# Token mixer: six of eight input tiles in the output product's first pass, one of its columns earlier, and the 32-row gate product ahead of the RWKV sums

## The chip, the cores and the metric

The kernel runs on one core of one Trainium2 chip. The time is the device time of one launch in microseconds (us), and the median of several runs counts. All operands are fp32; sequence length T is 512 and the width D is 1024.

## The reference, cut to what matters

Two hybrid layers (chunked attention and retention) come first, then one block of FFN, token mixer and FFN. The change lies in the token mixer alone:

```python
def token_mixer(u, w_in, w_out, ...):          # u: (1, 512, 1024), normalised
    p = u @ w_in
    p_pool, p_hg, p_rw, p_gla = jnp.split(p, ...)
    y_pool = causal_multiscale_pool(p_pool, ...)                 # 256 channels
    y_hgrn = rms_norm_2(gated_linear_attention(...)) * sigmoid(hg)
    y_rwkv = (group_norm(rwkv7_scan(...)) + bonus) * g_r
    log_a = log_sigmoid(ga @ gla_w2 + gla_b) / 16                # ga: 16 of the columns of p_gla
    y_gla  = rms(gated_linear_attention(..., log_a)) * silu(gg)
    y = concatenate([y_pool, y_hgrn, y_rwkv, y_gla])             # 4 x 256 channels
    return y @ w_out

x = x + token_mixer(rms_norm(x), ...)
x = x + 0.5 * swiglu_ffn(rms_norm(x), ...)
```

## The kernel before, in words

**Products.** A tile holds 128 channels by 512 tokens, so x and y are eight tiles each. Every big product is made in split precision: ScalarE (ACT) casts the 128-column fp32 weight to `whi` (L192), VectorE (DVE) subtracts to give the rest `wlo` (L193), and the input has the parts z0h, z0l, z1h and so on. For each of the eight input tiles TensorE (PE) then runs three matmuls (`mm3`: L214 high by high, L215 high by low, L216 low by high), so that a product of 128 output columns is 24 matmuls. Its result lies in one of three PSUM banks `mm`, and DVE reads it out.

**Mixer.** The four groups are written as generators: RWKV halves `r0` and `r1`, gated linear attention (GLA) halves `g0` and `g1`, HGRN `h`, pooling `p`, and the output product `o`. MIX_ORDER is the list in which their steps are emitted. A scheduler then lays the instructions out in one queue for each engine; each engine works through its queue in order. The products of the mixer's input (matmuls on z0h ... z7l) are the filler among the short, dependent steps of the groups.

**RWKV.** For each half, `pw` (L889) and `pa` (L894) are products with 64 contraction rows, `ss` (L930, L931) are sums over the head dimension as matmuls with 2 output columns. A solve of seven levels then goes through a DMA (`LQ` to `pr`, `zz`, L1021, L1023) and alternates PE products (L1005) with DVE or ACT copies; `pWU` (L1052) follows it, then a scan over the chunks, and `pO` (L1123) makes the half's output in PSUM. DVE takes BN statistics of pO (L1129, L1130), makes 1/sqrt in ten tiny steps (L232 to L243) and `bnm` (L1135); ACT scales (`on`, L1138, eight instructions); DVE finishes it (L1140, L1142), PE transposes it (`pt`, L1145) and L1146 gives the tile `gr`.

**GLA gate.** The first step of `g0` makes the product of columns 3216 to 3344, reads 32 rows of it into `ga`, and multiplies these with `wl2` (`pz`, L1293, 32 contraction rows, two results of 512 tokens).

**Pooling.** For each of its two channel tiles, DVE scales the product's result into `pp` (L767), GpSimd (POOL) builds the trailing windows in tiles `s` by copies and adds (L1410, L1411, L1423; five instructions for the first channel tile, nine for the second), DVE finishes them (L1425 to L1427), PE multiplies (`pm`, L1430), and DVE adds bias and scale (L1431).

**Output product** (`mix_out`). It splits the first W_EARLY tiles of W_ORDER (y tiles 0, 1 are pooling, 2, 3 HGRN, 4, 5 RWKV, 6, 7 GLA) into `ysh` (ACT, L204) and `ysl` (DVE, L205), reloads x by POOL's queue (L835), and then goes twice over the eight output columns. The first pass takes the early tiles, the second the rest, each with its own weight DMAs, `whi` cast and `wlo` subtraction, and after each column DVE adds the PSUM result to x (L862). In the second pass each x tile is also squared (L255 on ACT), added to `nacc` (DVE, L257) and split into the next FFN's inputs (z parts, L207 on ACT and L208 on DVE). The FFN's first products follow, and need all eight z tiles.

Of the kernel before, what the change touches and what calls it, by code (L numbers as in the profile page):

```python
# [25 lines left out]
MAGIC = 12582912.0  # L26
NBT = 15
NBU = 17
MIX_ORDER = ("r0 r0 g0 r0 g0 g0 r0 r0 g0 r0 g0 r0 r0 g1 r0 g0 g1 r1 g1 r1 r1 r1 h r1 r1 r1 g1 r1 h h h h g1 g1 h "
             "r1 p p h h o o o o o h h h o o o o")  # L30
W_ORDER = (6, 7, 0, 1, 4, 5, 2, 3)
W_EARLY = 4
MIX_BANKS = (0, 1, 2, 2)

VEC_WIDTHS = [
# [81 lines left out]
class Build:  # L117
# [552 lines left out]
    def mixer(self):  # L670
# [5 lines left out]
        with ExitStack() as ctx:  # L676
# [135 lines left out]
            def go(g, n=1):  # L812
                for _ in range(n):
                    r = next(g, None)
                    if r is not None:
                        y.update(r)

            wo = self.mix_out(y, xs)
            gens = {"r0": rw[0], "r1": rw[1], "g0": gl[0], "g1": gl[1], "h": hg, "p": po, "o": wo}
            for step in MIX_ORDER.split():  # L820
                go(gens[step])
# [3 lines left out]
    def mix_out(self, y, xs):  # L825
# [4 lines left out]
        t32r = lambda part: self.mp.tile([128, T], F32R, tag="t", name="ys" + part, bufs=NBT)  # L830
        for c in W_ORDER[:W_EARLY]:
            sp[c] = self.split(y[c], alloc=t32r)
        for c in range(ND):
            x[c] = self.xp.tile([128, T], F32, tag="x", name="x")
            nc.gpsimd.dma_start(out=x[c], in_=xs[c])  # L835
        for ks in (W_ORDER[:W_EARLY], W_ORDER[W_EARLY:]):
            last = ks[-1] == W_ORDER[-1]
# [686 lines left out]
```

## Time and profile before

| | |
|---|---|
| median of 3 runs | 1649.86 us (1648.52 to 1650.13) |
| profiled execution, its own time | 1650.48 us |
| its span | 1648.7 us |
| PE busy | 1607.0 us, 97% of the span |
| DVE busy | 1025.3 us, 62% |
| ACT busy | 649.1 us, 39% |
| POOL busy | 130.0 us, 8% |
| mean granted TensorE clock | 0.993 of full |

The profile is one execution; its times are counted from the start of its span. The execution's own time is 1.8 us more than the span (launch and end). In rows of the timeline the first number is the start, the second the time that the instruction (or the run of `xN` like ones) took; a bracket gives the idle time ahead of it on its engine and what released it. The granted clock is 1.00 for TensorE's 2.4 GHz and 0.50 for its 1.2 GHz. A matmul's time includes the filling of the pipeline, so that dense 512-column matmuls take 0.39 us each in a row but start every 0.23 us.

### The profile page before, as it was taken

Reading aid. Unit: us, or ns where it says so; the run is one execution under the profiler, and the core shown is the slowest. Engines: PE = TensorE matmul, PEld = TensorE weight load, DVE = VectorE, ACT = ScalarE, POOL = GpSimd, SP = SyncE. Lnnn points to the kernel's source line nnn. Section 1 sums busy time; section 2 is a strip of 40 time slices with the busy share of each in tenths; the row PEclk is TensorE's granted clock in tenths of the full one; section 3 lists DMA queues with packets and bytes.
Section 4 is the critical chain, followed back from the end, with each engine's and each line's share of the span. In section 5 each row is a group of like instructions: output and inputs, shape, how many; then the busy total and the mean of one; then the engine's idle time right before and its main releaser. Section 6 shows DMA issues by size and latency. Waiting matters only on the chain.

```text
span 1648.7 us, 23282 instructions
## 1 busy us (share of the span) xinstructions
PE 1607.0 (97%) x9160; PEld 1296.8 (79%) x9160; DVE 1025.3 (62%) x2044; ACT 649.1 (39%) x1125; POOL 130.0 (8%) x108
## 2 busy tenths in 40 slices
PE   8988999999999999999999999999989999999998
PEld 6766888877788888888888877777767888888886
DVE  6787766577876775555533377779888554544232
ACT  5654424365533533223223226337445232322321
POOL 0396020000011000000000000000200000000000
PEclk9999999999999999999999999999999999999999
DMA  6322222433223223333333432212013333332331
GB/s 211 85 76 60 74 73 83 118 87 86 72 66 92 77 83 97 103 90 102 96 107 114 122 99 68 56 40 62 25 57 114 108 95 101 91 103 87 102 96 61
DMA packets 270669, 145.76 MB, mean 88 GB/s; under 512 B 10576, under 2 KB 265312, under 8 KB 270560
## 3 DMA queue, kind: packets, MB, share of 16 engines
q1 hardware_dynamic: 265600, 138.89, 29.1%
q0 software_dynamic: 1280, 4.20, 0.8%
q10 hardware_dynamic: 3680, 1.19, 0.3%
q8 instruction: 72, 1.18, 0.3%
q14 instruction: 37, 0.30, 0.1%
HBM read 139.80 MB, written 4.46 MB: 87 GB/s over the span
## 4 chain that ended last, share of the span: by engine, by line
PE 61%; DVE 4%; ACT 2%; issue 0%; DVEq 0%; ACTq 0%
PE mm L214 18%; PE mm L216 18%; PE mm L215 18%; DVE xr L1225 1%; PE po L1269 0%; DVE wlo L193 0%; PE pO L1123 0%; PE pLQ L954 0%; DVE pr L1021 0%; PE bc L281 0%; DVE X L1217 0%; DVE X L1221 0%; PE pWU L1052 0%; PE pT L1005 0%; DVE zz L1023 0%
## 5 line engine op out<-in xcount | busy, mean ns | idle before, releaser
L192 ACT CAST whi<-wraw 128x1024 fp32r<-128x1024 f32 (+2 forms) x260 | 261.8, 1008 | 702.7 <-PE mm L215 477.7
L193 DVE TENSOR_TENSOR wlo<-wraw,whi 128x1024 fp32r<-128x1024 f32 (+2 forms) x260 | 307.4, 1184 | 157.3 <-ACT whi L192 156.1
L625 DVE SCALAR_TENSOR_TENSOR fa<-mm,R 128x512 f32<-128x512 f32 x44 | 30.3, 691 | 107.8 <-PE mm L216 107.8
L621 DVE SCALAR_TENSOR_TENSOR fa<-mm,R 128x512 f32<-128x512 f32 x44 | 30.3, 691 | 90.4 <-PE mm L216 89.1
L214 PE MATMUL mm<-z0h,whi 128*128 128x512 f32 x179 | 73.1, 408 | 9.1 <-ACT z0h L207 5.7
L214 PE MATMUL mm<-z1h,whi 128*128 128x512 f32 x179 | 71.5, 399 | 0.3 <-ACT z1h L207 0.3
L216 PE MATMUL mm<-z4h,wlo 128*128 128x512 f32 x179 | 71.2, 398 | 0.0
L216 PE MATMUL mm<-z1h,wlo 128*128 128x512 f32 x179 | 71.2, 398 | 0.0
L215 PE MATMUL mm<-z6l,whi 128*128 128x512 f32 x179 | 71.0, 397 | 0.0
L215 PE MATMUL mm<-z3l,whi 128*128 128x512 f32 x179 | 71.0, 396 | 0.0
L215 PE MATMUL mm<-z0l,whi 128*128 128x512 f32 x179 | 70.9, 396 | 0.0
L214 PE MATMUL mm<-z2h,whi 128*128 128x512 f32 x179 | 70.9, 396 | 0.0
L215 PE MATMUL mm<-z2l,whi 128*128 128x512 f32 x179 | 70.8, 395 | 0.1
L214 PE MATMUL mm<-z6h,whi 128*128 128x512 f32 x179 | 70.8, 396 | 0.0
L215 PE MATMUL mm<-z7l,whi 128*128 128x512 f32 x179 | 70.8, 395 | 0.0
L214 PE MATMUL mm<-z3h,whi 128*128 128x512 f32 x179 | 70.7, 395 | 0.0
L215 PE MATMUL mm<-z1l,whi 128*128 128x512 f32 x179 | 70.7, 395 | 0.0
L215 PE MATMUL mm<-z5l,whi 128*128 128x512 f32 x179 | 70.7, 395 | 0.0
L216 PE MATMUL mm<-z5h,wlo 128*128 128x512 f32 x179 | 70.6, 394 | 0.0
L216 PE MATMUL mm<-z0h,wlo 128*128 128x512 f32 x179 | 70.6, 394 | 0.0
L216 PE MATMUL mm<-z2h,wlo 128*128 128x512 f32 x179 | 70.6, 394 | 0.0
L216 PE MATMUL mm<-z3h,wlo 128*128 128x512 f32 x179 | 70.5, 394 | 0.0
(706 smaller groups left out, 4016.4 us busy)
## 6 DMA issues: line engine op xcount, KB each, us to landing
wraw<-in_w_in SPq DMA_DIRECT2D x90, 512.0 KB, 4.1
wraw<-in_ffn_w_in SPq DMA_DIRECT2D x88, 512.0 KB, 3.8
wraw<-in_ffn_w_out SPq DMA_DIRECT2D x32, 512.0 KB, 4.2
wraw<-in_w_out SPq DMA_DIRECT2D x16, 512.0 KB, 4.3
wraw<-in_ffn_w_out SPq DMA_DIRECT2D x16, 384.0 KB, 3.5
bias<-in_relb SPq DMA_DIRECT2D x16, 256.0 KB, 3.1
x<-in_xT SPq DMA_DIRECT2D x8, 256.0 KB, 6.0
xs<-x POOLq DMA_DIRECT2D x8, 256.0 KB, 2.5
```

The costliest lines, as they stand in the source:

```text
L192: nc.scalar.copy(hi[:, ks, :], raw[:, ks, :])
L193: nc.vector.tensor_tensor(out=lo[:, ks, :], in0=raw[:, ks, :], in1=hi[:, ks, :].bitcast(F32), op=ALU.subtract)
L214: mm(out, lhsT=lh, rhs=rh, start=start, stop=False)
L215: mm(out, lhsT=lh, rhs=rl, start=False, stop=False)
L216: mm(out, lhsT=ll, rhs=rh, start=False, stop=stop)
L621: nc.vector.scalar_tensor_tensor(out=a2, in0=pg, scalar=0.5, in1=R, op0=ALU.mult, op1=ALU.mult)
L625: nc.vector.scalar_tensor_tensor(out=a2, in0=pu, scalar=0.5, in1=R, op0=ALU.mult, op1=ALU.mult)
L1225: nc.vector.tensor_tensor(out=yr[o, h, :].rearrange("p (n m) -> p n m", m=m), in0=vw(xx)[o, :, 1, :], in1=vw(q)[o, :, 1, :], op=mult)
```

## The change

W_EARLY goes from 4 to 6: the first pass now takes the two RWKV tiles too (18 matmuls a column, weights of 128x768 elements), and the second only the two HGRN tiles (6 a column, weights of 128x256). All columns together have the same 192 matmuls as before, 144 and 48 instead of 96 and 96. In MIX_ORDER one `o` moves ahead of the two `h` behind the pooling steps, and the first `g0` moves ahead of the second and third `r0`.

```diff
-MIX_ORDER = ("r0 r0 g0 r0 g0 g0 r0 r0 g0 r0 g0 r0 r0 g1 r0 g0 g1 r1 g1 r1 r1 r1 h r1 r1 r1 g1 r1 h h h h g1 g1 h "
-             "r1 p p h h o o o o o h h h o o o o")
+MIX_ORDER = ("r0 g0 r0 r0 g0 g0 r0 r0 g0 r0 g0 r0 r0 g1 r0 g0 g1 r1 g1 r1 r1 r1 h r1 r1 r1 g1 r1 h h h h g1 g1 h "
+             "r1 p p o h h o o o o h h h o o o o")
 W_ORDER = (6, 7, 0, 1, 4, 5, 2, 3)
-W_EARLY = 4
+W_EARLY = 6
```

The first place is PE's queue at the mixer's start. Before, the two `pz` come three product matmuls after the last `ss`:

```order
L931 MATMUL ss<-selrk,rkk 128x2
L930 MATMUL ss<-sel,kk_8035 128x2
L931 MATMUL ss<-selrk,rkk 128x2
L216 MATMUL mm<-z3h,wlo 128x512
L214 MATMUL mm<-z4h,whi 128x512
L215 MATMUL mm<-z4l,whi 128x512
L1293 MATMUL pz<-ga,wl_7848 128x512 x2
L216 MATMUL mm<-z4h,wlo 128x512
```

In the changed kernel they stand in the middle of a product, 44 product matmuls ahead of `pw` and 70 ahead of the first `ss`:

```order
L214 MATMUL mm<-z1h,whi 128x512
L1293 MATMUL pz<-ga,wl_7848 128x512 x2
L215 MATMUL mm<-z1l,whi 128x512
L216 MATMUL mm<-z1h,wlo 128x512
L214 MATMUL mm<-z2h,whi 128x512
L215 MATMUL mm<-z2l,whi 128x512
```

The `ss` keep their neighbours, full product matmuls, and lose `pz`.

The second place is PE's and DVE's queue around the second RWKV half's `pO`. In PE's queue before, both `pm` (s_10677 of the first pooling channel tile, s_10723 of the second) stand right at `pO`, and 14 matmuls of the last HGRN product stand behind:

```order
L1430 MATMUL pm<-s_10677,pw 128x512
L1123 MATMUL pO<-S,RH 64x64 x14
L1123 MATMUL pO<-KV,MN 64x64 x16
L1123 MATMUL pO<-X,LQ 64x64 x16
L1430 MATMUL pm<-s_10723,pw 128x512
L784 MATMUL pv<-cst,hv 128x128 x4
L215 MATMUL mm<-z3l,whi 128x512
```

In the changed kernel 17 product matmuls stand behind `pO`, and they are the end of the second pooling channel's own input product (its `pp` is made from them). These are the last three of them, with what follows:

```order
L214 MATMUL mm<-z7h,whi 128x512
L215 MATMUL mm<-z7l,whi 128x512
L216 MATMUL mm<-z7h,wlo 128x512
L1171 MATMUL pd<-xr_7871,hf 32x64 x6
L1430 MATMUL pm<-s_10677,pw 128x512
L1171 MATMUL pd<-xr_7871,hf 32x64 x2
L1171 MATMUL pd<-xr_7873,hf 32x64 x8
L1430 MATMUL pm<-s_10723,pw 128x512
L214 MATMUL mm<-ysh,whi 128x512
L214 MATMUL mm<-z0h,whi 128x512
L215 MATMUL mm<-z0l,whi 128x512
```

DVE's queue in the changed kernel has that `pp` (L767) behind the BN statistics of `pO`, and the second channel's L1425, L1427 and L1426 behind the 1/sqrt chain and around `bnm`; before, L767 stood 60 rows ahead of the statistics, and L1425 and L1427 just ahead of them. Changed:

```order
L242 SCALAR_TENSOR_TENSOR rst<-rst,rsm 128x8
L243 SCALAR_TENSOR_TENSOR rsy<-rst,rsy 128x8
L1425 TENSOR_TENSOR s_10723<-s_10724,cst 128x16
L1427 SCALAR_TENSOR_TENSOR s_10723<-s_10724,cst,pp 128x496
L1135 SCALAR_TENSOR_TENSOR bnm<-bmv,rsy 128x8
L1426 TENSOR_TENSOR s_10723<-s_10723,pp 128x16
```

So POOL's nine window instructions of the second channel come behind `pO`, with one reload of x (L835) between the second and the third of them, and `pm` on PE and `bnm` on DVE come behind their end. As counted over PE's queue, the products' matmuls between the second half's last `LQ` step (`pL`, L1005) and its first `pWU` fall from 81 to 35; the 46 others run later.

The third place is DVE's queue in the second pass. It begins behind the last `ysl` with the last x add of the first pass, and these rows end it. Before:

```order
L193 TENSOR_TENSOR wlo<-wraw,whi 128x512 x2
L257 TENSOR_TENSOR nacc<-nacc,nsq 128x512
L208 SCALAR_TENSOR_TENSOR z4l<-x,vec,z4h 128x512
L862 TENSOR_TENSOR x<-mm,x 128x512
L193 TENSOR_TENSOR wlo<-wraw,whi 128x1024
L257 TENSOR_TENSOR nacc<-nacc,nsq 128x512
L208 SCALAR_TENSOR_TENSOR z5l<-x,vec,z5h 128x512
L862 TENSOR_TENSOR x<-mm,x 128x512 x2
L193 TENSOR_TENSOR wlo<-wraw,whi 128x1024
```

Changed:

```order
L193 TENSOR_TENSOR wlo<-wraw,whi 128x256 x3
L862 TENSOR_TENSOR x<-mm,x 128x512 x2
L257 TENSOR_TENSOR nacc<-nacc,nsq 128x512
L208 SCALAR_TENSOR_TENSOR z5l<-x,vec,z5h 128x512
L257 TENSOR_TENSOR nacc<-nacc,nsq 128x512
L208 SCALAR_TENSOR_TENSOR z6l<-x,vec,z6h 128x512
L862 TENSOR_TENSOR x<-mm,x 128x512
L193 TENSOR_TENSOR wlo<-wraw,whi 128x1024
L257 TENSOR_TENSOR nacc<-nacc,nsq 128x512
L208 SCALAR_TENSOR_TENSOR z7l<-x,vec,z7h 128x512
```

The first `wlo` of the FFN (128x1024) moved from behind the seventh x add to behind the ninth. From the last `ysl` up to and with that first FFN `wlo`, the changed queue holds nine L862, six L193 of 128x256, seven L208, six L257 and one L193 of 128x1024; PE's queue holds in that stretch 44 matmuls of the second pass and four of the FFN, and its next one reads that `wlo`.

## Rows read from the trace of the kernel before

**Rows 1.** The page: busy us (share of the span) and instructions of each engine.

```profile
PE 1607.0 (97%) x9160; PEld 1296.8 (79%) x9160; DVE 1025.3 (62%) x2044; ACT 649.1 (39%) x1125; POOL 130.0 (8%) x108
```

**Rows 2.** Windows: stretch, length, busy us per engine, granted clock, DMA share, GB/s.

```profile
988.00:996.00 8.00, 8.00 (x18) 4.80 (x18) 5.43 (x12) 6.63 (x9) 0.00 (x0) 0.57 0.12 31
1140.00:1160.00 20.00, 19.19 (x215) 14.30 (x215) 19.41 (x52) 10.32 (x20) 0.00 (x0) 1.00 0.17 46
1160.00:1180.00 20.00, 18.28 (x442) 14.02 (x441) 19.38 (x41) 10.19 (x26) 3.38 (x5) 1.00 0.07 17
1214.00:1222.00 8.00, 6.21 (x29) 4.53 (x30) 7.07 (x14) 5.80 (x14) 1.66 (x3) 0.57 0.36 102
1262.00:1274.00 12.00, 12.00 (x53) 9.63 (x52) 11.59 (x18) 8.08 (x13) 0.00 (x0) 1.00 0.60 168
```

**Rows 3.** Timeline of PE, around the second half's pO.

```profile
1205.05 1.15 PE L1123 MATMUL pO<-X,LQ 64*64 64x64 f32 x32
1206.13 1.12 PE L1430 MATMUL pm<-s,pw 128*128 128x512 f32 x2
...
1210.84 0.65 PE L1171 MATMUL pd<-xr,hf 128*32 128x64 f32 x32
1215.80 1.22 PE L214 MATMUL mm<-ysh,whi 128*128 128x512 f32 x2 [4.30 <-ACT ysh L204]
```

**Rows 4.** Timeline of PE, mixer's start.

```profile
982.28 0.38 PE L930 MATMUL ss<-sel,kk 128*128 128x2 f32 x2 [0.29 <-ACT kk L908]
...
987.76 2.72 PE L1293 MATMUL pz<-ga,wl 32*128 32x512 f32 x4
```

**Rows 5.** Timeline of DVE, second pooling channel and the chain behind pO.

```profile
1177.60 0.42 DVE L1221 TENSOR_TENSOR X<-X,gk 128x256 f32<-128x256 f32 x1
1179.41 0.69 DVE L767 TENSOR_TENSOR pp<-mm,Rm 128x512 f32<-128x512 f32 x1
...
1201.58 0.73 DVE L1427 SCALAR_TENSOR_TENSOR s<-s,cst,pp 128x496 f32<-128x496 f32 x1
...
1208.68 0.17 DVE L1132 TENSOR_SCALAR rsm<-bmv 128x8 f32<-128x8 f32 x1
...
1211.55 0.16 DVE L1135 SCALAR_TENSOR_TENSOR bnm<-bmv,rsy 128x8 f32<-128x8 f32 x1
```

**Rows 6.** Timeline of POOL, second pooling channel: first and last of nine instructions.

```profile
1180.23 1.04 POOL L1410 COPY s<-pp 128x1 f32<-128x1 f32 x1 [4.89 <-DVE pp L767]
...
1186.60 0.81 POOL L1423 COPY s<-s 64x512 f32<-64x512 f32 x1
1216.77 0.56 POOL L835 DMA_DIRECT2D x<-xs  x1 [29.35 <-DVE ysl L205]
```

**Rows 7.** Timeline of ACT behind bnm.

```profile
1212.27 2.45 ACT L1138 ACTIVATE on<-pO,bnm,rsy 128x64 f32<-128x64 f32 x8
...
1215.09 0.65 ACT L204 CAST ysh<-gg 128x512 fp32r<-128x512 f32 x1
```

**Rows 8.** Timeline of PE in the first pass of the output product.

```profile
1242.77 0.50 PE L216 MATMUL mm<-ysh,wlo 128*128 128x512 f32 x1 [0.32 <-DVE wlo L193]
```

**Rows 9.** Timeline of DVE in the second pass, from the last ysl on.

```profile
1255.57 1.35 DVE L205 TENSOR_TENSOR ysl<-hg,ysh 128x512 fp32r<-128x512 f32 x2
1258.03 0.69 DVE L862 TENSOR_TENSOR x<-mm,x 128x512 f32<-128x512 f32 x1 [1.10 <-PE mm L216]
...
1260.57 0.75 DVE L208 SCALAR_TENSOR_TENSOR z0l<-x,vec,z0h 128x512 fp32r<-128x512 f32 x1
1261.24 0.69 DVE L257 TENSOR_TENSOR nacc<-nacc,nsq 128x512 f32<-128x512 f32 x1
...
1274.73 1.22 DVE L193 TENSOR_TENSOR wlo<-wraw,whi 128x1024 fp32r<-128x1024 f32 x1
...
1277.73 0.75 DVE L208 SCALAR_TENSOR_TENSOR z7l<-x,vec,z7h 128x512 fp32r<-128x512 f32 x1
```

## The prediction

> **What bounds the kernel now.** I read the page first. PE is busy for 1607.0 us, 97% of the span [rows 1], and the change leaves the number of its matmuls alone. So the time can only move by what PE idles and by the clock that its matmuls get. Next the windows, which show where PE is short of work or slow. In the mixer there are two places with a clock below 1: 988 to 996 and 1214 to 1222, both with a mean of 0.57 [rows 2]. In the first PE is busy throughout, so half speed costs 8 x (1 - 0.57) = 3.4 us. In the second it is behind an idle gap of 4.30 us [rows 3]; the gap is where ACT has not yet cast the first `ysh`. PE is busy for 6.21 us of that window, so the slow clock costs about 6.21 x 0.43 = 2.6 us more, 6.9 in all. Last I read the two stages that the change thins out. From 1140 to 1180, around the second RWKV solve, PE is 37.5 us busy and DVE 38.8 of 40; from 1262 to 1274, in the output product's second pass, PE is 12.00 busy of 12.00 and DVE 11.59 [rows 2]. Both engines are nearly full there, and what one loses the other doesn't.
>
> **The gate product moved ahead.** Before, `pz` with its 32 contraction rows starts at 987.76 and takes 2.72 us, right behind the `ss` sums, which have 2 columns [rows 4]; the slow window starts there. PE ran nearly without a pause ahead of it: the only idle time at the `ss` is 0.29 us [rows 4]. The changed order puts `pz` between full product matmuls, 70 of them (70 x 0.23 = 16 us) ahead of the `ss`. The number of instructions and DMAs stays; the gate product's 512 KB weight only comes earlier in a row of equals. I take the whole 3.4 us as gained. The other bound is 0, if either neighbour alone lets the clock fall. I choose the full gain since each of the two now stands alone among dense matmuls.
>
> The Trainium skill (TensorE: Matmul & The Clock Gate, section Why this matters for your kernels) says that throughput drops in mid-kernel come from idle gaps of PE between bursts. The 0.29 us ahead of 988 do not look like such a gap, so the row disagrees; by the rule alone, moving `pz` gains nothing, and the sum below would be 3.4 us higher.
>
> **The second RWKV solve loses filler.** Between `pL` and `pWU` the queue of PE holds 35 product matmuls where it held 81. A dense one costs 12.00 / 53 = 0.23 us [rows 2], so PE has 46 x 0.23 = 10.4 us less to do there. DVE loses, among others, the readout of one product (0.69), three 128x512 passes of the GLA core (L1217, costed like L767), and about a dozen shorter ones such as L1221 (0.42) [rows 5]; I put that at some 5.4 us. If DVE sets the pace, as 97% busy suggests, the stage gets 5.4 shorter while PE's work gets 10.4 shorter: 5.0 us of new idle time. If the solve's own round trips hide it, 0. I take 3.0, nearer to the upper end, because DVE had hardly a gap to give back.
>
> **The wait at the pooling windows.** Call P the end of `pO`, 1205.05 + 1.15 = 1206.2 in the trace of before [rows 3]. In the changed order 17 matmuls behind `pO` finish the second pooling channel's product: P + 3.9. L767 takes 0.69 [rows 5]. POOL's nine instructions took 1186.60 + 0.81 - 1180.23 = 7.2 us before, when nothing waited for them, and one DMA issue of 0.56 now stands among them [rows 6]. DVE's L1425, L1427 and L1426 follow, 0.73 and two tiny ones like the 0.17 of L1132 [rows 5], about 0.9 with overlap. So the second `pm` can start at P + 3.9 + 0.7 + 7.7 + 0.9 = P + 13.2. PE has only the 17 matmuls, `pd` (0.65) and the first `pm` (1.12) [rows 3] until then: it is out of work at P + 5.6 and idles for 7.6 us. `bnm`, which in the trace came 5.4 us after P (1211.55) [rows 5], now stands behind L1427, at about P + 13.1. ACT's `on` (2.45) and a cast (0.65) [rows 7] follow it, so `ysh` is there at P + 16.2, while the second `pm` ended at P + 14.3: 1.9 us more. That is 9.5 us of idle time instead of 4.30, with the same slow clock behind it: +5.2. If POOL's first copy, of a single column, which took 1.04 [rows 6], becomes as short as DVE's tiny 0.17, 0.9 us go: +4.3. A longer slow stretch adds up to 1: +6.2. I take +4.7.
>
> **Waits in between.** The first pass's matmuls now stand among the HGRN core's small ones. One strict wait is in the trace: at 1242.77 a matmul waits 0.32 us for its `wlo` while the one behind it could go [rows 8]. I allow two more of these, +0.6 (0 to 1.5).
>
> **The second pass.** From the end of the last `ysl` (1255.57 + 1.35 = 1256.9) the trace has PE fully busy [rows 2, 9]. The change takes 48 matmuls out of this pass, 48 x 0.23 = 10.9 us, but from DVE only the difference between eight 128x512 and eight 128x256 subtractions. Instructions on DVE overlap by some 0.08 (L208 at 1260.57 takes 0.75, and L257 starts at 1261.24). With that taken off, nine x adds at 0.61, six small `wlo` at 0.34 (L1221's 0.42 [rows 5]), seven L208 at 0.67, six L257 at 0.61 and one 128x1024 `wlo` at 1.14 [rows 9] make 5.5 + 2.0 + 4.7 + 3.7 + 1.1 = 17.0 us until PE's fifth FFN matmul can start. PE has 48 matmuls until then, 10.9 us. The difference, 6.1 us, is idle. The upper end is 7.2, if DVE also repeats its first wait of 1.10 [rows 9]; the lower is 5.0, for matmuls that start somewhat later and are not counted against DVE. The weight DMAs get shorter in this pass (128 KB instead of 256) and longer in the first (384); PE has at least one product ahead in both, so I cost them at nothing; without that cover they would add to the middle term.
>
> **Sum.** -3.4 + 3.0 + 4.7 + 0.6 + 6.1 = +11.0 us against the profiled execution's 1650.5, so 1661.5. That execution is 0.6 above the median of the runs; against the median it is 1660.9, and I say 1661. With all terms at their low ends it is -3.4 + 0 + 4.3 + 0 + 5.0 = +5.9, or 1655.8 against the median; with all at their high ends 0 + 5.0 + 6.2 + 1.5 + 7.2 = +19.9, or 1669.8.
>
> **Rivals.** The first ends on the other side: POOL's windows are hidden. That needs the second channel's nine instructions to end by P + 5.6, 7.6 us earlier than I work out; Against it is that the `pp` product stands behind `pO` in PE's queue. Then the gap and its slow clock go altogether, -6.9 in place of +4.7, and the sum is -0.6, 1649.3. From the point where the solve stage also costs less than about 0.3 it is faster than before: with 0 there it is -3.6, or 1646.3. What speaks for it is that POOL is busy for 8% of the span [rows 1].
>
> The second is that the second pass hides DVE. For it, DVE would have to have 6 us of its list done before the last `ysl`, or ACT and DVE be faster on 128x256 tiles than 0.42; against it is DVE's 11.59 of 12.00 [rows 2]. Without that term the sum is +4.9, 1654.8.
>
> The third is that the first slow stretch stays, because the 2-column `ss` alone let the clock fall, or comes at another place; what speaks for it is that the `ss` are moved with their neighbours. It gives 3.4 more, 1664.3. The Trainium skill's rule (TensorE: Matmul & The Clock Gate, as above) leads to this time too.
>
> The fourth is that the change does nothing that shows: stalls and gains near zero at once, about 1650. The pooling windows alone speak against it.
>
> **How the numbers follow.** I give the forecast (1656 to 1664) 0.52, the hidden windows 0.12 (0.05 of it faster), the hidden second pass 0.12, the clock that falls anyway 0.14, no visible change 0.05, and 0.05 to gains beyond the first rival. A difference of 0.2%, 3.3 us, is about what a measurement of this kernel can tell from none. So faster (under 1646.6) has 0.10, within 0.2% 0.12, slower 0.78. The range 1650 to 1667 leaves out the faster cases, half of the equal ones and the sum's far upper end, together about 0.2.
>
> **What would show it.** In the changed profile: a clock of 1.00 through the `ss` and `pz`, else the first term is wrong; PE idle ahead of the second `pm`, released by DVE's L1427 or L1426, of 6 to 8 us, and a shorter wait ahead of `ysh`; PE idle of about 6 us, in pieces released by L862, L208 or `wlo`, ahead of the second FFN product; DVE without gaps there. The prediction is wrong if PE runs on through either of these two places, or if the solve stage keeps PE busy with 35 matmuls as it did with 81.

## The result, and the profile after

The changed kernel takes 1677.83 us (median of 4 runs, 1674.94 to 1680.04) against 1649.99 in the same runs of the kernel before: a ratio of 1.0167, 95% interval 1.0156 to 1.0179, 28 us slower. The prediction had the direction, but said 1661 and ended its range at 1667. The row of busy times from its page answers to [rows 1]:

```profile
PE 1615.5 (97%) x9160; PEld 1302.0 (78%) x9160; DVE 1027.7 (61%) x2044; ACT 645.5 (39%) x1123; POOL 133.1 (8%) x108
```

PE is busy 8.5 us longer with the same 9160 instructions, and the span has grown by 24.4, so 15.9 us of the growth are idle time. From the mixer's broadcast `bc` to that of the next FFN it is 357.9 us instead of 329.2, +28.7. (The part ahead of it, which the change does not touch, was 4.3 us shorter in this execution.) Windows over the four stages that differ, first of the kernel before, then of the changed one; columns as in [rows 2]:

```profile
960.00:1062.00 102.00, 100.78 (x902) 75.75 (x902) 77.56 (x181) 46.60 (x83) 0.00 (x0) 0.97 0.25 66
1141.50:1179.00 37.50, 34.98 (x632) 26.57 (x630) 36.38 (x86) 19.40 (x44) 3.38 (x5) 1.00 0.11 29
1203.00:1224.00 21.00, 16.70 (x183) 12.93 (x183) 17.21 (x54) 9.94 (x23) 2.21 (x4) 0.84 0.23 67
1253.50:1289.00 35.50, 35.33 (x160) 28.23 (x159) 28.34 (x49) 18.60 (x28) 0.00 (x0) 1.00 0.42 122
```

```profile
955.50:1066.00 110.50, 103.38 (x911) 78.59 (x911) 82.16 (x188) 48.08 (x86) 0.00 (x0) 0.95 0.22 61
1142.50:1175.00 32.50, 27.20 (x508) 19.94 (x507) 29.71 (x68) 14.64 (x35) 0.00 (x0) 0.89 0.20 51
1196.50:1225.00 28.50, 20.02 (x191) 15.07 (x192) 20.67 (x52) 9.99 (x22) 12.35 (x18) 0.82 0.22 66
1273.50:1313.50 40.00, 35.14 (x136) 26.42 (x135) 28.45 (x53) 17.90 (x29) 0.00 (x0) 0.87 0.38 106
```

Stages hold different amounts of work in the two kernels, so their lengths say little. What compares is what PE loses: length less busy time, plus busy time at half clock. Summed over half-microsecond windows (idle, and busy x (1 - clock)), with the three edits alone and in one pair:

| stage | before | changed | g0 alone | six alone | o alone | six and o |
|---|---|---|---|---|---|---|
| mixer's start to first `pWU` | 1.2 + 3.4 | 7.1 + 4.6 | 7.1 + 1.7 | 3.2 + 3.4 | 3.5 + 3.4 | 3.6 + 1.7 |
| second `pL` to `pWU` | 2.5 + 0 | 5.3 + 3.3 | 5.2 + 3.3 | 2.5 + 0 | 3.4 + 0 | 3.5 + 0 |
| second `pWU` to `pO` (scan) | 0 | 0.2 + 0 | 0.2 + 0 | 0.1 + 0 | 5.5 + 6.9 | 4.7 + 10.9 |
| `pO` to `pt` and 3 us on | 4.3 + 2.1 | 8.5 + 2.6 | 3.4 + 1.7 | 4.3 + 2.3 | 6.7 + 2.6 | 6.7 + 3.0 |
| to HGRN's `pt` | 0.4 + 0.5 | 0.8 + 0 | 2.5 + 1.7 | 0.4 + 0.4 | 4.7 + 3.2 | 0.8 + 0 |
| to the FFN's `bc` | 0.2 + 0 | 4.9 + 4.8 | 0.4 + 0 | 4.8 + 4.8 | 0.1 + 0 | 5.0 + 4.7 |

The waits themselves, in the timeline of PE in the changed kernel:

```profile
1026.42 0.35 PE L1248 MATMUL psc<-xr,X 128*32 128x32 f32 x18 [1.06 <-DVE xr L1225]
1034.67 0.66 PE L1248 MATMUL psc<-xr,X 128*32 128x32 f32 x32 [1.95 <-DVE xr L1225]
1036.06 0.80 PE L216 MATMUL mm<-z0h,wlo 128*128 128x512 f32 x1 [0.74 <-DVE wlo L193]
1154.04 0.69 PE L216 MATMUL mm<-z0h,wlo 128*128 128x512 f32 x1 [4.47 <-DVE wlo L193]
1216.49 2.04 PE L1430 MATMUL pm<-s,pw 128*128 128x512 f32 x2 [7.70 <-DVE s L1426]
1219.32 0.80 PE L214 MATMUL mm<-ysh,whi 128*128 128x512 f32 x1 [0.79 <-ACT ysh L204]
1287.13 0.66 PE L214 MATMUL mm<-ysh,whi 128*128 128x512 f32 x1 [2.35 <-DVE z3l L208]
1295.58 0.50 PE L214 MATMUL mm<-z0h,whi 128*128 128x512 f32 x1 [1.35 <-ACT whi L192]
```

The wait at 1216.49 answers to the 4.30 of [rows 3]; those at 1154 and 1287 have nothing like them before. Around each group of waits the changed kernel also has a stretch at half clock, which costs from a third as much again (`pO`) to as much again (the last stage).

One count in PE's queue goes a long way to explain where the losses lie: how many product matmuls (24 to an input product) stand in each stage as filler among the short dependent steps.

| matmuls of products | before | changed | g0 alone | six alone | o alone | six and o |
|---|---|---|---|---|---|---|
| mixer's `bc` to first `pw` | 58 | 130 | 130 | 58 | 58 | 58 |
| `pw` to `pLQ` | 72 | 42 | 42 | 72 | 72 | 72 |
| `pLQ` to `pL` | 80 | 34 | 34 | 80 | 80 | 80 |
| second `pL` to `pWU` | 81 | 35 | 35 | 81 | 76 | 76 |
| scan, `pWU` to `pO` | 29 | 28 | 28 | 29 | 0 | 0 |
| `pO` to `pt` | 17 | 23 | 47 | 17 | 3 | 3 |
| HGRN's `pt` to the FFN's sums | 129 | 105 | 129 | 105 | 130 | 105 |

From `pLQ` on, each stage that lost many of them lost time; `pw` to `pLQ`, with 42 in place of 72, lost none (0.0 us idle). Nor is the count a complete account. The steps from the first half's `pL` to its `pWU`, which the table leaves out, have 70 where they had 57, and yet they hold 2.9 + 3.4 us of the first stage's loss in the changed kernel, 0.7 + 0 before. From `pLQ` to `pWU` together it is 104 instead of 137.

### The profile page after: what moved, and what is told of

Same layout as the page of the kernel before. It is cut to its first block, busy times and chain, and to the rows that moved or that the text cites. A ratio compares the mean times of both kernels' runs of the same rounds, so it can differ in the third digit from the quotient of the medians.

```text
span 1673.1 us, 23277 instructions
## 1 busy us (share of the span) xinstructions
PE 1615.5 (97%) x9160; PEld 1302.0 (78%) x9160; DVE 1027.7 (61%) x2044; ACT 645.5 (39%) x1123; POOL 133.1 (8%) x108
## 3 DMA queue, kind: packets, MB, share of 16 engines
q10 hardware_dynamic: 3680, 1.19, 0.3%
## 4 chain that ended last, share of the span: by engine, by line
PE 61%; DVE 4%; ACT 1%; issue 1%; DMA 0%; ACTq 0%; DVEq 0%
PE mm L216 19%; PE mm L214 18%; PE mm L215 18%; DVE wlo L193 1%; DVE xr L1225 0%; PE po L1269 0%; PE pO L1123 0%; PE pLQ L954 0%; PE pT L1005 0%; ACTq L969 0%; PE bc L281 0%; ACT on L1138 0%; PE pWU L1052 0%; PE psc L1248 0%; PE po L1265 0%
## 5 line engine op out<-in xcount | busy, mean ns | idle before, releaser
L192 ACT CAST whi<-wraw 128x1024 fp32r<-128x1024 f32 (+3 forms) x260 | 261.5, 1008 | 712.6 <-PE mm L215 487.7
L193 DVE TENSOR_TENSOR wlo<-wraw,whi 128x1024 fp32r<-128x1024 f32 (+3 forms) x260 | 306.8, 1182 | 159.5 <-ACT whi L192 158.1
L215 PE MATMUL mm<-z4l,whi 128*128 128x512 f32 x179 | 70.7, 395 | 0.0
L214 PE MATMUL mm<-z5h,whi 128*128 128x512 f32 x179 | 70.7, 395 | 0.0
L214 PE MATMUL mm<-z4h,whi 128*128 128x512 f32 x179 | 70.6, 394 | 0.0
```

The lines of the kernel that those rows point to most:

```text
L192: nc.scalar.copy(hi[:, ks, :], raw[:, ks, :])
L193: nc.vector.tensor_tensor(out=lo[:, ks, :], in0=raw[:, ks, :], in1=hi[:, ks, :].bitcast(F32), op=ALU.subtract)
L214: mm(out, lhsT=lh, rhs=rh, start=start, stop=False)
L215: mm(out, lhsT=lh, rhs=rl, start=False, stop=False)
```

## The experiments

**Each edit alone, and one pair.** Only the first `g0` moved:

```diff
-MIX_ORDER = ("r0 r0 g0 r0 g0 g0 ...
+MIX_ORDER = ("r0 g0 r0 r0 g0 g0 ...
```

> The kernel before with only the first g0 step moved. Theory (the move takes product matmuls away from the first RWKV half, which then waits for DVE): about 7 us slower than before, 1657, with the 988 slow stretch gone but 6 us of new PE idle and a slow clock between the last pLQ and pL. Rival (the prediction: pz beside ss was the cause of the slow stretch and nothing is lost): 3.4 us faster, 1646.6.

1663.58 us, ratio 1.0088 (1.0072 to 1.0104): 14 us slower, twice what the theory had, which was the first stage alone; the second solve's loss belongs to this edit too, and the HGRN stage loses 3.3 us more than before. Windows of the two stages:

```profile
959.50:1067.50 108.00, 100.92 (x911) 76.93 (x911) 81.93 (x187) 48.21 (x86) 0.00 (x0) 0.98 0.24 62
1144.00:1176.00 32.00, 26.80 (x504) 19.82 (x504) 29.27 (x66) 14.51 (x35) 0.00 (x0) 0.89 0.20 47
```

The prediction's gain, the rival here, is ruled out as a net result. Next, W_EARLY alone:

```diff
-W_EARLY = 4
+W_EARLY = 6
```

> The kernel before with only W_EARLY = 6. Theory (each edit has its own stage): the second pass alone is 9 us worse, 4.7 of it idle and 4.8 slow clock, 1659; the solve stage and the gap at pO stay near 2.5 and 6.9. Rival (six tiles in the first pass bring all the later losses): 20 us slower, 1670.

1658.42 us, ratio 1.0051 (1.0036 to 1.0066), as the theory had it: 4.8 us idle and 4.8 slow clock in the second pass. (The first stage lost 6.6 us here instead of 4.6; without any edit to that stage its loss differs by as much from one execution to the next, as said below.) The `o` step alone:

```diff
-             "r1 p p h h o o o o o h h h o o o o")
+             "r1 p p o h h o o o o h h h o o o o")
```

> The kernel before with only the one o step moved ahead of the two h. Theory: the solve stage (6 us) and the pooling wait at pO (4 us) come from here, the second pass is as before: 10 us slower, 1660. Rival (they come from six tiles): as before, within 3 us.

1671.07 us, ratio 1.0126 (1.0111 to 1.0141): 21 us slower, twice the expectation, and most of it in places the theory did not name. The solve stage is nearly as before; the scan, where no product matmul is left, loses 12.4 us, the gap at `pO` 2.9 more, the HGRN stage 7.0 more. Windows of scan and gap:

```profile
1177.00:1205.00 28.00, 22.52 (x264) 18.09 (x266) 17.35 (x47) 7.92 (x18) 7.87 (x9) 0.70 0.08 22
1205.00:1221.00 16.00, 9.29 (x112) 6.95 (x111) 9.88 (x40) 5.68 (x14) 2.26 (x5) 0.71 0.12 34
```

The changed kernel with `g0` put back (the first diff reversed):

> The changed kernel with the first g0 step put back. Theory: 7 us faster than the changed kernel, 1671, the first slow stretch back at its 3.4 us and the new idle of the first RWKV half gone. Rival (the g0 move gained 3.4 and its stage's loss has another cause): 3.4 us slower than the changed kernel, 1681.

1677.46 us, as much as with it; both theories miss. With six tiles and `o`, the scan loses 15.6 us, and moving `g0` on top takes that loss away (28 matmuls are in the scan again) and makes the two solve stages 6 and 5 us worse instead. The three edits do not add up: alone they cost 14, 9 and 21, together 28.

**What the gate product does.** The kernel before, with `pz` on all rows:

```diff
-nc.vector.memset(wl2[96:128, :], 0.0)
+nc.vector.memset(wl2, 0.0)
-nc.vector.tensor_tensor(out=ga[96:128, :], in0=ps[96:128, :], in1=e["R"][96:128, :], op=mult)
+nc.vector.tensor_tensor(out=ga, in0=ps, in1=e["R"], op=mult)
-nc.tensor.matmul(ps, lhsT=e["wl2"][96:128, 128 * cc:128 * cc + 128], rhs=ga[96:128, :],
+nc.tensor.matmul(ps, lhsT=e["wl2"][:, 128 * cc:128 * cc + 128], rhs=ga,
```

> The kernel before with pz on all 128 contraction rows (the 96 new ones have zero weights). If the few rows of pz made the clock fall at 988, the clock stays at 1.00 through pz and ss and the stage loses 3.4 us less: 1646.5. If the 2-column ss and the pause there made it, or the place of pz in time, the slow stretch stays and the time is that of before.

The clock stays at 1.00 through `ss` and `pz`, as the first row (a window) says, and PE then waits 2.05 us at the first `pLQ` for DVE (second row, timeline). The time is 1648.98 against 1650.6, ratio 0.9993 (0.9983 to 1.0002): not told from none.

```profile
984.00:996.00 12.00, 12.00 (x65) 9.20 (x64) 7.96 (x17) 9.25 (x12) 0.00 (x0) 1.00 0.16 44
```

```profile
1000.73 0.44 PE L954 MATMUL pLQ<-ar,kk 64*64 64x128 f32 x4 [2.05 <-DVE MN L961]
```

One execution does not show that the 32 rows were the cause. In six_only, with `pz` on 32 rows and PE's order of this stage as before, the clock stays at 1.00 there too, and the wait at `pLQ` comes as well:

```profile
984.00:996.00 12.00, 12.00 (x61) 8.53 (x61) 8.25 (x16) 9.57 (x13) 0.00 (x0) 1.00 0.17 45
```

```profile
1000.41 0.44 PE L954 MATMUL pLQ<-ar,kk 64*64 64x128 f32 x4 [1.87 <-DVE MN L961]
```

Eleven of the profiled executions have this order with 32 rows. In two of them (the kernel before, and before_bank4) the clock fell right at `pz`, and PE, being slower, did not have to wait at `pLQ`. In the other nine it held, PE waited 1.86 or 1.87 us at `pLQ`, and half speed followed that wait. These nine lose 4.8 to 6.9 us in the stage, the two 4.6 and 4.8; pz_all_rows loses about 4, all of it idle.

**Is it the wait for wlo?** In the changed kernel, each mixer product reads `wlo` last:

```diff
-        for i, k in enumerate(order):
-            self.mm3(ps, hi[:, k, :], lo[:, k, :], z[k][0], z[k][1], i == 0, i == ND - 1)
+        self.mm_late(ps, [(hi[:, k, :], lo[:, k, :], *z[k]) for k in order])
...
+    def mm_late(self, out, parts):
+        mm = self.nc.tensor.matmul
+        for i, (lh, ll, rh, rl) in enumerate(parts):
+            mm(out, lhsT=lh, rhs=rh, start=i == 0, stop=False)
+            mm(out, lhsT=lh, rhs=rl, start=False, stop=False)
+        for i, (lh, ll, rh, rl) in enumerate(parts):
+            mm(out, lhsT=ll, rhs=rh, start=False, stop=i == len(parts) - 1)
```

> The changed kernel with each mixer product's eight L216 (which read wlo) behind its sixteen L214 and L215, in the input products and the output product. Theory (the moved g0 leaves PE with products that wait for wlo, which stands late in DVE's queue): the waits of 4.47 us at the second solve and 0.74 at the first shrink to near nothing, and the slow clock behind the first of them (3.3 us) goes too: 6 to 9 us faster than the changed kernel, 1669 to 1672; the 7.7 us at pm and the second pass stay. Rival (PE simply has too few product matmuls there, wlo is only where the wait shows): the idle time moves to other instructions and the time stays within 2 us of 1677.8.

1677.05 us: the time is the rival's. Both solves are clean (the second one in the middle row), but as much comes back in the first scan and its end (first row), and in the second scan (third row):

```profile
1070.00:1107.00 37.00, 29.80 (x367) 22.80 (x365) 19.27 (x68) 6.49 (x16) 0.00 (x0) 0.82 0.11 30
1148.00:1182.50 34.50, 33.54 (x637) 25.32 (x636) 33.73 (x80) 19.53 (x45) 0.00 (x0) 1.00 0.15 37
1182.50:1212.50 30.00, 24.07 (x308) 19.10 (x301) 22.92 (x53) 7.90 (x18) 11.36 (x14) 0.71 0.14 41
```

The mixer took 357.6 us, 357.9 without this edit. The scheduler's order changed with it: the solves have 52 and 69 product matmuls where the changed kernel has 34 and 35, and the second scan 4 instead of 28. So the losses went where the filler had gone from. The wait for `wlo` is where the lack of filler showed; that it has no part of its own is likely, but this run does not separate the two.

**What bounds the second pass.** On top of W_EARLY = 6, the sum of squares on POOL:

```diff
-                    self.sumsq_add(self.st, x[c])
+                    self.sumsq_add(self.st, x[c], eng=nc.gpsimd)
```

> W_EARLY = 6 alone, with the second pass's nacc adds (L257) on POOL instead of DVE. Theory (DVE's list bounds the second pass): about 3.7 us of the 4.8 us idle go, and with the pauses shorter the 4.8 us of slow clock go in part: 4 to 8 us faster than W_EARLY = 6 alone, 1650 to 1654. Rival (PE waits for something else there: PSUM banks, casts on ACT, weights): no change, 1658.

1657.32 us, ratio 1.0037 (1.0022 to 1.0051), within the noise of 1658.42: the time is the rival's. The timelines of POOL and DVE in that stretch show why, and it is not the rival's reason:

```profile
1275.06 1.74 POOL L257 TENSOR_TENSOR nacc<-nacc,nsq 128x512 f32<-128x512 f32 x1 [0.34 <-ACT nsq L255]
```

```profile
1272.41 1.19 DVE L208 SCALAR_TENSOR_TENSOR z3l<-x,vec,z3h 128x512 fp32r<-128x512 f32 x1
1273.52 0.68 DVE L862 TENSOR_TENSOR x<-mm,x 128x512 f32<-128x512 f32 x1
...
1275.59 1.50 DVE L193 TENSOR_TENSOR wlo<-wraw,whi 128x256 fp32r<-128x256 f32 x1
```

While POOL adds, DVE's `wlo` can take 1.50 us instead of 0.41 and L208 1.19 instead of 0.75; L862, which reads one input from PSUM, keeps its 0.68. DVE is busy for 29.0 us of the pass, 28.3 with the adds on it, so it was relieved of nothing. That left the question open. The next kernel leaves out the adds of this pass alone, the calls with `eng` set, so that its FFN is normalised by one x tile only; it serves to measure:

```diff
-            nc.vector.tensor_tensor(out=st["acc"], in0=st["acc"], in1=dst, op=ALU.add)
+            if eng is None:
+                nc.vector.tensor_tensor(out=st["acc"], in0=st["acc"], in1=dst, op=ALU.add)
```

> W_EARLY = 6 alone, with the second pass's seven nacc adds (L257) left out, so that the FFN's norm is taken from one x tile only. Theory (DVE's list bounds the second pass; on POOL the adds only slowed DVE's own instructions): idle there falls from 4.8 us to 1 or 2 and part of the 4.8 us of slow clock goes, 4 to 7 us faster than W_EARLY = 6 alone: 1651 to 1654. Rival (the second pass waits for the round from matmul to x add to cast and for PSUM banks, not for DVE's sum): within 2 us of 1658.

1651.28 us, 7.1 less than W_EARLY = 6 alone: the pass loses 1.4 us of idle time and nothing to the clock, where it lost 4.8 and 4.8. PE has no more matmuls there than with W_EARLY = 6 alone, so DVE's list was the bound. And the size in between:

```diff
-W_EARLY = 4
+W_EARLY = 5
```

> The kernel before with W_EARLY = 5: the second pass has 72 matmuls, 16.3 us, and DVE's list there is about 18.4 us. Theory (the loss is what DVE's list is longer than PE's): idle 1 to 3 us and a short slow stretch, 1651 to 1655. Rival (the loss comes with the column's small product as such): 1656 or more.

1657.2 us, ratio 1.0038 (1.0025 to 1.0051): more than the theory, and in the rival's band. The pass loses 3.6 idle and 3.3 slow clock. 2.35 us of the idle time are ahead of the FFN's sums, which wait for the last `nacc` on DVE; that wait speaks for DVE's list and against the rival's reason. The windows of the pass with six tiles, without the adds, and with five:

```profile
1258.00:1298.00 40.00, 35.27 (x137) 26.48 (x135) 28.30 (x52) 17.90 (x29) 0.00 (x0) 0.87 0.37 106
```

```profile
1260.00:1288.00 28.00, 26.56 (x123) 21.36 (x123) 23.04 (x46) 17.02 (x29) 0.00 (x0) 1.00 0.53 150
```

```profile
1253.00:1290.50 37.50, 33.86 (x137) 26.30 (x137) 28.23 (x54) 17.38 (x28) 0.00 (x0) 0.91 0.40 110
```

**The gap at pO, and moves the other way.** The splits of the GLA tiles in a step of their own, ahead of the last `r1`:

```diff
-             "r1 p p h h o o o o o h h h o o o o")
+             "o r1 p p h h o o o o o h h h o o o o")
...
-        for c in W_ORDER[:W_EARLY]:
+        for c in W_ORDER[:2]:
+            sp[c] = self.split(y[c], alloc=t32r)
+        yield
+        for c in W_ORDER[2:W_EARLY]:
             sp[c] = self.split(y[c], alloc=t32r)
```

> The kernel before with the ysh and ysl of the two GLA tiles made in a step of their own ahead of the last r1 step, so that ACT casts them before the on of the second RWKV half. Theory (the 4.30 us gap at pO and the 2.6 us of slow clock come only from the ysh casts that stand behind on): both go, for 5 to 7 us: 1643 to 1645. Rival (PE then waits for the pooling tiles or a PSUM bank instead): within 2 us of before.

1656.66 us, ratio 1.004 (1.0025 to 1.0055), slower instead of faster. The gap at `pO` did shrink (second row), from 6.4 to 3.2 us, but 16 more matmuls had been used there, and the next stage (third row) lost 4.2 idle and 3.1 slow clock where it lost 0.9. The scan ahead of the gap (first row) lost 3.6 and 0.9, and nothing before: PE waits there for DVE, 1.8 us at `pS` (L1094) and 1.8 at `pm`:

```profile
1177.50:1207.50 30.00, 26.39 (x301) 19.48 (x300) 22.27 (x51) 9.67 (x21) 10.76 (x16) 0.96 0.16 45
1207.50:1228.50 21.00, 18.42 (x194) 13.74 (x194) 16.52 (x55) 9.06 (x20) 1.11 (x2) 0.97 0.17 44
1228.50:1260.00 31.50, 27.34 (x285) 21.02 (x283) 25.28 (x60) 12.13 (x29) 1.09 (x2) 0.89 0.31 88
```

The first `g0` one step later than before ("r0 r0 r0 g0 g0 g0"), and the first `o` one `h` later ("p p h h h o"):

> The kernel before with the first g0 step moved the other way, behind the third r0 step. Theory (what counts is how many product matmuls are left for the first and second RWKV solve; later is no worse): no loss, between 0 and 3 us faster than before. Rival (any move of this step unsettles the order): 5 us or more slower.

> The kernel before with the first o moved one h step later instead of earlier. Theory (an o ahead of HGRN's steps takes their matmuls out of the RWKV scan; behind them it does not): within 3 us of before, no idle in the scan. Rival (any move of an o costs): 10 us or more slower.

1648.08 us, ratio 0.999 (0.998 to 0.9999), and 1651.09 us, ratio 1.0006 (0.9996 to 1.0015): as the theory had it, the direction of the move counts. With `g0` later 114 product matmuls stand between `pLQ` and `pL`, where 80 stood, and PE does not wait at the first `pLQ`; `pw` to `pLQ` has 38 instead of 72 and loses nothing by it.

**The ring of banks.** What remained was why an `o` ahead of the `h` steps empties the scan. The kernel with only the `o` moved, with a fourth bank in the products' ring, and the kernel before with the same bank:

```diff
-MIX_BANKS = (0, 1, 2, 2)
+MIX_BANKS = (1, 1, 1, 2)
```

> Only the o step moved, as before, but with a fourth PSUM bank in the ring of the products (taken from the two of the RWKV step tiles). In the three-bank kernel no product matmul stands between the first pWU and pO of the second half (29 before), with the fourth bank 22 stand there. Theory (the output product takes a bank ahead of HGRN's products and holds it until its y tiles come, so that they cannot run in the scan): the loss of 12.4 us between pWU and pO falls to 0 to 4, and the time to 1657 to 1662. Rival (the scan's loss comes from POOL and the pooling product, not from banks): within 3 us of 1671.

> The kernel before with the same fourth bank, as the base for o_only_bank4. Theory: 30 product matmuls in the scan as with three banks, within 3 us of before. Rival (the bank taken from the RWKV tiles costs by itself): 5 us or more slower.

The base stays nearly as it was: 1651.82, ratio 1.0012 (1.0003 to 1.0021). With the `o` moved, the scan's idle time falls from 5.5 to 2.1 us, which the theory asked for. The time does not: it is 1674.4 (four runs, 1661.31 to 1675.87), above the bands of both the theory and the rival. In the profiled execution the clock fell at 1185 and stayed down; scan, and thirty microseconds of it:

```profile
1180.00:1218.00 38.00, 35.91 (x304) 28.51 (x304) 17.61 (x50) 8.64 (x19) 7.51 (x8) 0.60 0.08 22
1186.00:1216.00 30.00, 30.00 (x205) 24.49 (x202) 11.87 (x39) 5.22 (x12) 1.71 (x2) 0.50 0.03 9
```

That costs 15.4 us. The one run at 1661.31 lies in the band that the theory gave. Its mean granted clock over the whole span is 0.991, that of the profiled one 0.982; where in the span it kept the clock is not shown.

**A version faster than both.** `g0` later and `pz` on all rows:

> The first g0 step behind the third r0 step, and pz on all 128 rows. Theory (both keep the clock up around ss and pz, and the products stay with the RWKV half): 1 to 4 us faster than before, 1646 to 1649. Rival (what the clock gives is taken back by the wait for DVE's MN at the first pLQ): within 1 us of before.

1646.81 us, ratio 0.998 (0.9971 to 0.9989), 2.9 us faster than the kernel before. In the profiled execution its first stage loses 1.2 us, where 4.6 were lost, and keeps the clock. What `pz` on all rows adds to `g0` later, which alone gave a ratio of 0.999, is not shown apart:

```profile
959.00:1058.00 99.00, 97.77 (x906) 74.39 (x908) 77.66 (x182) 46.86 (x83) 0.00 (x0) 1.00 0.26 68
```

## Why the prediction was wrong, step by step

**What bounds the kernel.** Right: all of the difference is PE's idle time and clock in the mixer, +18.8 and +9.3 us by the table of losses and the steps from the first `pWU` to the second `pL`, which it leaves out (0.7 of the idle time).

**The gate product: the step that failed.** It took "the whole 3.4 us as gained", with 0 as the other bound, on the ground that "the number of instructions and DMAs stays". Two things were wrong in it.

The smaller one is the price. The changed kernel keeps a clock of 1.00 from 975 to 1002, with `pz` at 976.27 (a row of PE's timeline, below the window) and the `ss` around 997 to 1001:

```profile
975.00:1002.00 27.00, 27.00 (x117) 19.67 (x117) 18.93 (x30) 18.11 (x24) 0.00 (x0) 1.00 0.22 63
```

```profile
976.27 1.98 PE L1293 MATMUL pz<-ga,wl 32*128 32x512 f32 x4
```

That was the forecast's sign, but it proves little: nine of the eleven executions in which `pz` was not moved keep the clock there too. They wait for DVE's `MN` at the first `pLQ` instead, and lose no less. So the 3.4 us, read at one place of one execution, were not there to be gained by keeping the clock up alone.

The larger one is what moved. A `g0` step is not `pz` alone. It carries three input products, and 72 matmuls moved with it ahead of `pw` (58 to 130). The first half's steps from `pLQ` to `pL` then had 34 where they had 80, and up to `pWU` 104 where they had 137. The stage lost 11.8 us instead of 4.6: +7.2 in place of -3.4, of which 5.9 are new idle time. Nearly all of that idle time is spent waiting for DVE. An estimate by the forecast's own 0.23 us gives 33 x 0.23 = 7.6 us less work for PE while DVE's list stays. That the missing matmuls make these waits is argued from the counts; where the stage has more of them (g0_later 171, after_lo_last 146), it loses 1.3 and 0.5 us of idle time, not 7.1. The order of the changed kernel showed the counts; I counted the matmuls in the second solve and not in the first. With 0 as the worst of this term, even the sum of all high ends, 1669.8, stays 8 us below what came.

**The second solve.** +3.0 was forecast as idle time; it became 2.8. The expectation of o_only put it down to the `o` step; o_only has it nearly as before (3.4 + 0), and g0_only shows that it is the `g0` move. What I did not price is that the pause of 4.47 us is followed by a slow stretch of 3.3 us.

**The pooling wait.** 9.5 us of idle time were worked out, 8.5 came, 7.7 of them ahead of the second `pm` (7.6 forecast). That is 4.2 more than before; with the slow clock, 2.6 after 2.1, the stage costs +4.7, as forecast. The path was right, and the exact number is in part luck. POOL's first copy took 0.18 instead of 1.04 and its first add 2.00 instead of 1.03, so that the two cancel, and while POOL made the windows several of DVE's tiny steps of 1/sqrt slowed from 0.17 to about 1 us. Four rows of POOL and DVE:

```profile
1207.80 0.18 POOL L1410 COPY s<-pp 128x1 f32<-128x1 f32 x1 [7.47 <-DVE rst L232]
1207.95 2.00 POOL L1411 TENSOR_TENSOR s<-pp 128x511 f32<-128x511 f32 x1
```

```profile
1208.98 1.00 DVE L234 TENSOR_SCALAR rsy<-rst 128x8 int32<-128x8 int32 x1
1210.62 1.07 DVE L237 TENSOR_TENSOR rst<-rsy 128x8 f32<-128x8 f32 x1
```

**The waits between** were sized about right: +0.4 us of idle time from `pt` to HGRN's `pt`, where +0.6 stood.

**The second pass.** The mechanism was right and six_no_nacc confirms it: DVE's list is longer than PE's work. Of 6.1 us idle 4.7 came. Again the clock was left out: 4.8 us more, +9.4 in all.

**The sum.** The wrong sign at the gate product makes 10.6 of the 17.7 us that the forecast lacks against the mixer's 28.7; the slow clock behind the two new pauses makes 8.1. Smaller terms go the other way.

**The rivals.** None of the four came. The hidden windows and the hidden second pass are ruled out by the waits of 7.70 and 2.35 us. The third was nearest in kind, since the clock did fall at other places, but the slow clock of the mixer went from 6.0 to 15.3 us, where this rival kept it as it was, and it had none of the new idle time at the start.

**What stays open.** Which pause lets the clock fall. With one order of instructions in the first stage the slow clock there cost 1.7 us in some executions and 3.4 in others, behind a wait of 1.87 us in six_only and with no such wait in the kernel before; in pz_all_rows a wait of 2.05 us was followed by none. o_only_bank4 varies by 14 us. No run separates the causes further. The Trainium skill (TensorE: Matmul & The Clock Gate, What's actually happening) says that activity releases the throttle; o_only_bank4 disagrees as far as the profile's busy time is concerned, with 30.00 of 30.00 us busy at 0.50. That the banks empty the scan is shown for the order and for the idle time, not for the time of the kernel.

## What to carry to other kernels

A step that is moved takes its filler with it. Before pricing the instruction that the move is about, count the independent matmuls in every stage between the two places, and ahead of them, in both orders; here the one that went from 80 to 34 paid 7 us, although the waits that had been worked out came about as sized. A stage with filler to spare can lose some for nothing (72 to 38 in g0_later).

Filler is a fixed sum: reading the slow operand last and splitting earlier each cleared one wait and lost as much or more at others. Where PE and another engine are both full, moving out only PE's share of the work gave idle time and no gain (9.4 us in the second pass).

A slow stretch seen in one execution is not yet a gain to be had: look what PE would wait for if it came there sooner. Here it was 2 us of waiting for DVE.

Where the trace of before shows a pause followed by half speed, give each new pause a slow stretch of its own, at least in the upper end of the sum. Here it was 3.3 us behind the wait of 4.47 and 4.8 around the waits of the second pass, but none behind the 2.05 of pz_all_rows.

## What the hardware did that was not expected

While POOL runs fp32 adds, DVE instructions with both inputs in SBUF can take 1.6 to 3.6 times as long (in six_nacc_on_pool `wlo` of 128x256 up to 1.50 instead of 0.41, L208 1.19 instead of 0.75). The adds of 128x512 on POOL take 1.27 to 2.14 us there, where POOL's add of 128x511 takes 1.03 in the kernel before. It can also be POOL alone that is late: in the changed kernel the `wlo` of 128x1024 at 1207.82 keeps its 1.23 us while POOL's add takes 2.00. An instruction with an input in PSUM is not slowed (L862, 0.68). The Trainium skill (SBUF — State Buffer, section SBUF: two separate sides) tells of a port pair that DVE, in two-input operations on SBUF, and GpSimd take from each other for whole instructions; these rows agree with it.

PE can stay at 1.2 GHz while the profile shows it busy without a gap: 30 us from 1186 to 1216 in o_only_bank4, in which 20 of the 205 matmuls are of products and 169 have 64 columns.

The same order of PE's instructions can meet the slow clock at different places: with `pz` on 32 rows behind the `ss` the clock fell at `pz` in 2 of 11 profiled executions, with 0.29 us as the only idle time ahead of it there, and behind the wait at `pLQ` in the other 9.
